# A hybrid decoder step with features on partitions in memory: input rows, gains, y and k without transpositions

## The chip, the cores and the metric

The kernel runs on one core of one Trainium2 chip. The time is the device time of one execution in microseconds. Engines are named as the profile names them: PE is TensorE's matrix multiply and PEld its weight load, DVE is VectorE, ACT is ScalarE, POOL is GpSimd, SP is SyncE, which issues most of the DMAs.

## The reference

One layer for two groups of rows that share all weights: a prompt of 256 rows and 8 samples of 4 rows, 288 rows (T) in all, each of D = 2048 features.

```
h   = RMSNorm(x, g_pre)
q, k, v, u, vg = split(h @ w_in)          # q, k rotated on the first quarter of each head of 128
A   = block-sparse attention(q, k, v)     # the samples also read 2048 cached keys and values each
B   = gelu(u) * (tril(w_spatial[g]) @ LayerNorm(gelu(vg)) + b_spatial[g])
mix = (sigmoid(h @ Wga) * (A @ w_a_out) + sigmoid(h @ Wgb) * (B @ w_b_out)) @ w_o
x   = x + RMSNorm(mix, g_post)
x   = x + RMSNorm(SwiGLU(RMSNorm(x)), g_pof)
y   = x + (p @ w_ple) * sigmoid(RMSNorm(x) @ w_ple_gate)
```

The outputs are y, the rotated k rows, the v rows and the normalised vg rows of the samples. Everything is float32.

## The kernel before

Inside the kernel every activation lies with features on partitions: a tile is 128 features by 288 rows. The inputs and outputs lie in memory by rows, so x, p, the gains, the spatial weights, y and k are turned on PE. Each transposition is one PE instruction with the identity matrix `cst`; a PSUM tile `pt` takes three (two of 128 prompt rows, one of 32 sample rows padded to 128).

**Products.** `product` (lines 237 to 260) does all the large multiplications. It takes 256 output features at a time. For each group of 4 blocks of 128 input features SP loads 512 KB of weights into one of four `wr` buffers, ACT rounds them to `wh`, DVE makes the remainder `wl`, and PE does three multiplications of 128 x 288 for each block and half: `wh` by the high part, `wh` by the low part, `wl` by the high part of the activation. There are 520 such weight groups.

**Start.** SP loads `cst` (line 134), then x in four chunks of 512 features, three tiles each (line 157); ACT loads `g_pre` in 16 rows (line 165), POOL the five other gains (line 168) after clearing the sample tiles (lines 139, 140). Ten multiplications of ones (`wake`, line 185) start PE, two PE instructions each. `h_parts` (209) turns one block into `pt`; ACT writes `hh` = g * x (215) and DVE the remainder `hl` (216) from PSUM. Two q products run along, one weight group each per chunk. `square_sums` (218) squares the untransposed rows on ACT; `r0_of` (226) makes the reciprocal root of the mean square with three diagonal matrices on PE. `rope` (300) then empties the q accumulators; it needs `r0`.

**k, v and the cache.** `k_gen` (331) turns each k tile back to rows through `to_tokens` (310: three transpositions, an ACT copy, a DVE copy) and POOL stores them (322, 323). Cached keys and values (2 MB per round of four pages) stream in on SP during some 550 us; their PE work is woven into the products by planned counts.

**Spatial weights.** `prep_gen` (458) loads them in rows of 512 bytes (462), turns eight 128 x 128 blocks on PE (469) and masks them on DVE from PSUM (470).

**Middle.** After the `w_a_out` products x is loaded again (855 to 864): four chunks `xc` with two buffers, 48 transpositions, 16 DVE copies into `x1`. The `w_o` products follow, then `p` is loaded and turned (933 to 947), which `le_products` need, then `norm_of` and `residual`.

**End.** The last products `pg` have the epilogue `pg_done` (1031). After each second group of 256 features it turns 512 features of the result with 12 transpositions (1045), copies them on ACT (1047) and stores three pieces on SP (1048).

**Order.** The framework sets the order on each engine and each DMA queue at build time, from a simulation of when operands and buffers are ready, in program order where several are. Each engine and each queue then works through its list in order: a wait holds up what stands behind it.

Of the kernel before, what the change touches and what calls it, by code (L numbers as in the profile page):

```python
# [21 lines left out]
NB = 8  # L22
# [86 lines left out]
def tile_hybrid_step(ctx: ExitStack, tc: tile.TileContext, a: dict, o: list):  # L109
    nc = tc.nc  # L110
    y_p, y_s, kp_o, vp_o, ks_o, vs_o, gv_o = o
# [20 lines left out]

    cst = perm.tile([128, 128], F32, name="cst")
# [8 lines left out]
    TP = 3 * 128  # L142

    def turn(pt, tiles, c):

        for j, t in enumerate(tiles):
            nc.tensor.transpose(pt[:, j * 128:j * 128 + 128], t[:, c], ident)

    xp = a["x_prompt"].rearrange("b s d -> (b s) d")
    xs = a["x_sample"].rearrange("b s d -> (b s) d")  # L150
    srcs = [(xp[0:128], 128), (xp[128:256], 128), (xs, TS)]
    XC = 512
    x_tok = [[p_x0.tile([128, XC], F32, name=f"x{j}_{c}") for j in range(3)] for c in range(D // XC)]

    def x_load(c):
        for (src, n), t in zip(srcs, x_tok[c]):
            nc.sync.dma_start(t[:n], src[:, c * XC:c * XC + XC])

    for tiles in x_tok:
        clear_rows(tiles[2])  # L160
    x_load(0)
    names = ["g_pre_mix", "g_post_mix", "g_pre_ffn", "g_post_ffn", "g_ple", "g_vnorm"]
    glist = [a[name].rearrange("l (k p) -> (l k) p", p=128) for name in names]
    gl0 = p_x0.tile([16, 128], F32, name="gl0")
    nc.scalar.dma_start(gl0, glist[0])
    gl = p_x0.tile([72, 128], F32, name="gl")
    for i, g in enumerate(glist[1:]):
        nc.gpsimd.dma_start(gl[16 * i:16 * i + g.shape[0]], g)
# [11 lines left out]
    def bank(shape, name, of="aux"):  # L180
        return psum[of].tile(shape, F32, name=name, tag=of)
# [27 lines left out]
    def h_parts(c):  # L209
        for i in range(XC // 128):  # L210
            k = c * (XC // 128) + i
            pt = bank([128, TP], "pt")
            turn(pt, x_tok[c], slice(i * 128, i * 128 + 128))
            pt = pt[:, :T]
            nc.scalar.activation(hh[:, k], pt, AF.Copy, scale=g_pre[:, k:k + 1])
            nc.vector.scalar_tensor_tensor(hl[:, k], pt, g_pre[:, k:k + 1], hh[:, k], op0=ALU.mult, op1=ALU.subtract)

    def square_sums(c):
        for j in range(3):
            junk = p_x0.tile([128, XC], F32, name="junk", bufs=2)  # L220
            nc.scalar.activation(junk, x_tok[c][j], AF.Square, accum_out=sums[:, j, c:c + 1])

    sums = p_x0.tile([128, 3, D // XC], F32, name="sums")
    r0 = p_h.tile([128, T], F32, name="r0")

    def r0_of():
        st = p_x0.tile([128, 3], F32, name="st")
        nc.vector.tensor_reduce(st, sums, axis=AX.X, op=ALU.add)
        r0p = bank([128, TP], "r0p")
        for j in range(3):  # L230
            dg = p_x0.tile([128, 128], F32, name="dg", bufs=3)
            nc.vector.tensor_scalar(dg, ident, st[:, j:j + 1], None, op0=ALU.mult)
            nc.tensor.matmul(r0p[:, j * 128:j * 128 + 128], ones_d, dg, start=True, stop=True)
        rstd_of(r0, r0p[:, :T], p_x0.tile([128, T], F32, name="r0t"))
# [40 lines left out]
    for c in range(D // XC):  # L275
        h_parts(c)
        for q in q2:
            next(q)
        if c + 1 < D // XC:
            x_load(c + 1)  # L280
        square_sums(c)
    r0_of()
    gains = turned_gains(gl, 72)
    g_pm, g_pf, g_pof, g_pl, g_vn = (gains[:, 16 * i:min(16 * i + 16, 72)] for i in range(5))
# [46 lines left out]
    def k_gen():  # L331
        def done(x, h):
            rope(kT[:, h:h + 2], x)
            c = p_a.tile([128, 2, GC], F32, name="k_tok", tag="a2", bufs=2)
            cs = p_a.tile([TS, GC], F32, name="ks_tok", tag="a3")
            for t in range(2):
                s = slice(t * HD, t * HD + HD)
# [93 lines left out]
    def gmlp_gen():  # L431
# [26 lines left out]
        def prep_gen():  # L458
            gm = p_g.tile([128, C_GM], F32, name="gm")
            nc.sync.dma_start(gm, a["c_gm"])  # L460
            wsp = p_g.tile([128, H, 128], F32, name="wsp", tag="vn")
# [3 lines left out]
            tri = gm[:, C_TRI:C_TRI + 128][:, None, :].to_broadcast([128, 4, 128])  # L465
            for g in range(0, H, 4):
                tp = bank([128, 4, 128], "wt")
                for t in range(4):
                    nc.tensor.transpose(tp[:, t], wsp[:, g + t], ident)
                nc.vector.tensor_tensor(wst[:, g:g + 4], tp, tri, ALU.mult)  # L470
                yield 0.5
# [382 lines left out]

    p_xt, end_xt = pool("p_xt", "left")
    for c in range(4):
        xc = [p_xt.tile([128, 512], F32, name=f"xc{j}", bufs=2) for j in range(3)]
        clear_rows(xc[2])
        for (src, n), t in zip(srcs, xc):
            nc.sync.dma_start(t[:n], src[:, c * 512:c * 512 + 512])  # L860
        for k in range(4):
            pt = bank([128, TP], "pt")
            turn(pt, xc, slice(k * 128, k * 128 + 128))
            nc.vector.tensor_copy(x1[:, 4 * c + k], pt[:, :T])
# [68 lines left out]
    pp_ = a["p_prompt"].rearrange("l b s c -> (l b s) c")  # L933
    ps_ = a["p_sample"].rearrange("l b s c -> (l b s) c")
    psrc = [(pp_[0:128], 128), (pp_[128:256], 128), (ps_, TS)]
    p_tok = [p_n.tile([128, PLE], F32, name=f"ptok{j}", tag="yt", bufs=3) for j in range(3)]
    clear_rows(p_tok[2])
    for (src, n), t in zip(psrc, p_tok):
        nc.sync.dma_start(t[:n], src)
    ph = p_n.tile([128, 2, T], F32R, name="ph")  # L940
    pl = p_n.tile([128, 2, T], F32R, name="pl")
    for k in range(2):
        pt = bank([128, TP], "pt")
        turn(pt, p_tok, slice(k * 128, k * 128 + 128))
        pt = pt[:, :T]
        nc.scalar.copy(ph[:, k], pt)
        nc.vector.tensor_tensor(pl[:, k], pt, ph[:, k], ALU.subtract)
# [15 lines left out]
    end_xt.close()  # L963
# [14 lines left out]
    for half in range(2):  # L978
# [40 lines left out]
        for g in range(8):  # L1019
# [8 lines left out]
    outs = [y_p.rearrange("b s d -> (b s) d")[0:128], y_p.rearrange("b s d -> (b s) d")[128:256],  # L1028
            y_s.rearrange("b s d -> (b s) d")]

    def pg_done(x, g):
        for t in range(2):
            m = 2 * g + t
            gt = p_f.tile([128, T], F32, name="pgt", tag="fs", bufs=4)
            nc.vector.tensor_tensor(gt, x[t], r3, ALU.mult)
            nc.scalar.activation(gt, gt, AF.Sigmoid)
            nc.vector.tensor_tensor(gt, gt, le[:, m], ALU.mult)
            nc.vector.tensor_tensor(x1[:, m], x1[:, m], gt, ALU.add)
        if g % 2 == 0:
            return  # L1040
        for j in range(3):
            n = 128 if j < 2 else TS
            pt = bank([128, 512], "yt")
            for i in range(4):
                nc.tensor.transpose(pt[:n, i * 128:i * 128 + 128], x1[:, 2 * g - 2 + i, j * 128:j * 128 + n], ident)
            yt = p_n.tile([128, 512], F32, name="yt", bufs=3)
            nc.scalar.copy(yt[:n], pt[:n])
            nc.sync.dma_start(outs[j][:, (g // 2) * 512:(g // 2) * 512 + 512], yt[:n])
# [5 lines left out]
    for end in (end_f, _x, end_z, end_n, end_banks):  # L1054
# [3 lines left out]
_INS = ["x_prompt", "x_sample", "cache_k", "cache_v", "page_table", "p_prompt", "p_sample", "g_pre_mix", "w_in",  # L1058
        "g_vnorm", "w_spatial", "b_spatial", "w_a_out", "w_b_out", "w_gate", "w_o", "g_post_mix", "g_pre_ffn",
        "w_ffn_in", "w_ffn_out", "g_post_ffn", "g_ple", "w_ple_gate", "w_ple"]  # L1060
_OUTS = [(1, SEQ, D), (NB, NS, D), (1, 1, SEQ, H, HD), (1, 1, SEQ, H, HD), (1, NB, NS, H, HD), (1, NB, NS, H, HD),
         (1, NB, NS, H * 128)]
# [25 lines left out]
```

## Time and profile before

| | us |
|---|---|
| median of 3 runs | 1848.33 (1846.85 to 1848.41) |
| the profiled execution | 1845.0 |
| its span, first to last instruction | 1843.2 |
| PE busy in the span | 1822.8 (99%) |
| DVE, ACT, POOL busy | 951.8, 775.2, 97.8 |
| granted TensorE clock, mean | 0.997 |

The span is 1.8 us shorter than the execution it belongs to. Multiplications overlap in the pipeline: one of 128 x 288 is listed with 295 ns, but the next one starts 133 ns later, so busy time is not a sum of steps, and the step from one start to the next is what an instruction costs PE. Of the runs, the profiled execution is the shortest.

### The profile page before, as it was taken

The page shows a single profiled execution, that of the slowest core. Times are in us where ns is not written, and L with a number is a line of the kernel's source. Part 1 is how long each engine was busy: PE and PEld are TensorE (multiplying, and loading weights), DVE is VectorE, ACT ScalarE, POOL GpSimd, SP SyncE. Part 2 cuts the span into 40 slices and gives each one's busy share as a digit, 9 for nine tenths or more (in the row PEclk, how much of TensorE's full clock was granted, in tenths as well). Part 3 has the DMA queues.
Part 4 walks back from the last instruction along what each step waited for, and adds up shares of the span by engine and source line. Part 5 has one row for each costly group of instructions (what it writes and reads, how often), then busy time and mean ns, then how long its engine had stood idle before and what let it go on. Part 6 is the DMA issues. An engine that isn't in the chain of part 4 may idle for free.

```text
span 1843.2 us, 38883 instructions
## 1 busy us (share of the span) xinstructions
PE 1822.8 (99%) x16004; PEld 1775.4 (96%) x16004; DVE 951.8 (52%) x1357; ACT 775.2 (42%) x1090; POOL 97.8 (5%) x195
## 2 busy tenths in 40 slices
PE   8999999999999999999999999999999999999898
PEld 8999899999999989999999999999999999999898
DVE  4754446544444347635855554433545545444764
ACT  5334455434333344445533333333333333434643
POOL 2010112000000000110000000000000000001000
PEclk9999999999999999999999999999999999999999
DMA  9589999999999985544555554445555555444452
GB/s 344 168 297 350 329 354 329 365 344 363 356 340 353 374 280 180 181 164 138 167 162 170 162 170 162 163 163 166 172 162 170 162 170 162 164 161 155 137 192 101
DMA packets 312673, 414.83 MB, mean 225 GB/s; under 512 B 13544, under 2 KB 275296, under 8 KB 312496
## 3 DMA queue, kind: packets, MB, share of 16 engines
q1 hardware_dynamic: 311120, 409.23, 64.7%
q8 instruction: 125, 2.05, 0.4%
q0 software_dynamic: 1200, 2.76, 0.4%
q10 hardware_dynamic: 176, 0.37, 0.1%
q14 instruction: 52, 0.43, 0.1%
HBM read 407.45 MB, written 4.85 MB: 224 GB/s over the span
## 4 chain that ended last, share of the span: by engine, by line
PE 97%; DVE 1%; ACT 1%; issue 0%; DMA 0%; SPq 0%; DVEq 0%
PE f L256 5%; PE f L257 5%; PE fa L257 5%; PE f L255 5%; PE fg L257 5%; PE fg L255 5%; PE fg L256 5%; PE fa L255 5%; PE fa L256 5%; PE values L732 3%; PE scores L634 3%; PE ga L255 2%; PE pg L255 2%; PE gb L255 2%; PE ga L256 2%; PE pg L257 2%
## 5 line engine op out<-in xcount | busy, mean ns | idle before, releaser
L249 DVE TENSOR_TENSOR wl<-wr,wh 128x1024 fp32r<-128x1024 f32 (+1 forms) x520 | 623.9, 1201 | 719.9 <-ACT wh L248 708.1
L248 ACT CAST wh<-wr 128x1024 fp32r<-128x1024 f32 (+1 forms) x520 | 535.8, 1031 | 896.0 <-PE f L256 165.2
L257 PE MATMUL f<-dh,wl 128*128 128x288 f32 x704 | 208.9, 297 | 0.0
L256 PE MATMUL f<-dl,wh 128*128 128x288 f32 x704 | 208.5, 296 | 0.0
L255 PE MATMUL f<-dh,wh 128*128 128x288 f32 x704 | 207.5, 295 | 0.0
L255 PE MATMUL fg<-zh,wh 128*128 128x288 f32 x704 | 207.3, 295 | 0.0
L257 PE MATMUL fg<-zh,wl 128*128 128x288 f32 x704 | 207.2, 295 | 0.0
L257 PE MATMUL fa<-zh,wl 128*128 128x288 f32 x704 | 206.7, 295 | 0.5 <-DVE wl L249 0.5
L256 PE MATMUL fa<-zl,wh 128*128 128x288 f32 x704 | 206.0, 294 | 0.9 <-DVE zl L925 0.9
L256 PE MATMUL fg<-zl,wh 128*128 128x288 f32 x704 | 206.9, 294 | 0.0
L255 PE MATMUL fa<-zh,wh 128*128 128x288 f32 x704 | 204.7, 295 | 1.0 <-ACT zh L924 1.0
L256 PEld LDWEIGHTS fa<-zl,wh 128*128 128x128 f32 x704 | 132.5, 188 | 1.2 <-DVE zl L925 1.2
L257 PEld LDWEIGHTS fa<-zh,wl 128*128 128x128 f32 x704 | 132.0, 188 | 0.7 <-DVE wl L249 0.7
L256 PEld LDWEIGHTS fg<-zl,wh 128*128 128x128 f32 x704 | 132.7, 188 | 0.1
L256 PEld LDWEIGHTS f<-dl,wh 128*128 128x128 f32 x704 | 132.6, 188 | 0.0
L255 PEld LDWEIGHTS fa<-zh,wh 128*128 128x128 f32 x704 | 131.4, 188 | 1.2 <-ACT zh L924 1.2
L255 PEld LDWEIGHTS f<-dh,wh 128*128 128x128 f32 x704 | 132.3, 188 | 0.1
L255 PEld LDWEIGHTS fg<-zh,wh 128*128 128x128 f32 x704 | 132.3, 188 | 0.0
L257 PEld LDWEIGHTS fg<-zh,wl 128*128 128x128 f32 x704 | 132.1, 188 | 0.1
L257 PEld LDWEIGHTS f<-dh,wl 128*128 128x128 f32 x704 | 132.1, 188 | 0.1
L255 PE MATMUL pg<-zh,wh 128*128 128x288 f32 x256 | 76.1, 304 | 5.4 <-ACT zh L924 5.4
L255 PE MATMUL gb<-hh,wh 128*128 128x288 f32 x256 | 76.7, 299 | 0.0
(356 smaller groups left out, 3792.2 us busy)
## 6 DMA issues: line engine op xcount, KB each, us to landing
wr<-in_w_ffn_in SPq DMA_DIRECT2D x176, 512.0 KB, 3.4
kt<-in_cache_k SPq DMA_DIRECT2D x128, 512.0 KB, 7.4
vt<-in_cache_v SPq DMA_DIRECT2D x128, 512.0 KB, 6.5
wr<-in_w_in SPq DMA_DIRECT2D x80, 512.0 KB, 6.3
wr<-in_w_ffn_out SPq DMA_DIRECT2D x80, 512.0 KB, 3.2
wr<-in_w_gate SPq DMA_DIRECT2D x64, 512.0 KB, 6.8
wr<-in_w_o SPq DMA_DIRECT2D x32, 512.0 KB, 3.2
wr<-in_w_ple_gate SPq DMA_DIRECT2D x32, 512.0 KB, 3.2
```

The source lines that it names most:

```text
L248: nc.scalar.copy(wh[:, :m], raw[:, :m])
L249: nc.vector.tensor_tensor(wl[:, :m], raw[:, :m], wh[:, :m], ALU.subtract)
L255: nc.tensor.matmul(accs[t], wh[:, i, c], xh, start=k == 0, stop=False)
L256: nc.tensor.matmul(accs[t], wh[:, i, c], xl, start=False, stop=False)
L257: late["mm"] = nc.tensor.matmul(accs[t], wl[:, i, c], xh, start=False, stop=k == n - 1)
L634: i = nc.tensor.matmul(sp[b][32 * g:32 * g + 32, 4 * n:4 * n + 4], Q[:, h2, g, dq], kt[:, :, c:c + 32], start=h2 == 1 and dq == 0, stop=h2 ...
L732: i = nc.tensor.matmul(oa[b][32 * g:32 * g + 8], w[:, n, 32 * g + 8 * part:32 * g + 8 * part + 8], v[:, :, g], start=first and part == 3, ...
```

## The change

The host passes x, p, the gains and the spatial weights with features (or the summed index) on partitions, and takes y and k in that form; it turns them itself. In the kernel all 182 transpositions of full tiles and the 2 small ones of the gains go away, with the copies that emptied them. The identity stays; v and vg are still turned.

- x: four loads of 128 x 1152 (4.6 KB per partition, 576 KB each); `hh` and `hl` read x from SBUF. `squares` works on the turned tile, 1152 elements wide, in place on ACT, and DVE adds the chunks; `r0_of` has two PE multiplications by ones.
- gains: one load of 128 x 88 (352 bytes per partition) on ACT's queue, ahead of x; `cst` moves from SP's queue to POOL's.
- k: one POOL store of 128 x 576 per group, straight from `kT`.
- spatial weights: loaded straight into `wst`, masked in place by one DVE operation of 128 x 1024.
- x again: one load of 2.36 MB into `x1` on SP; p: one load of 128 x 576, one ACT and one DVE operation.
- y: a store of 128 x 576 on SP after each group of 256 features, eight in all.

```diff
@@ start
+    xs = [p_x0.tile([128, XK, T], F32, name=f"x{c}") for c in range(KD // XK)]
+    def x_load(c):
+        nc.sync.dma_start(xs[c], a["x"][:, c * XK:c * XK + XK])
+    gains = perm.tile([128, 88], F32, name="gains")
+    nc.scalar.dma_start(gains, a["gains"])
+    x_load(0)
-    nc.sync.dma_start(cst, a["c_perm"][:, :128])
+    nc.gpsimd.dma_start(cst, a["c_perm"][:, :128])
...
-            pt = bank([128, TP], "pt")
-            turn(pt, x_tok[c], slice(i * 128, i * 128 + 128))
+            nc.scalar.activation(hh[:, k], xs[c][:, i], AF.Copy, scale=g_pre[:, k:k + 1])
...
+    def squares(c):
+        nc.scalar.activation(xs[c], xs[c], AF.Square)
+        if c:
+            nc.vector.tensor_tensor(xs[0], xs[0], xs[c], ALU.add)
...
+        nc.vector.tensor_tensor(q[:, 0:2], q[:, 0:2], q[:, 2:4], ALU.add)
+        for i in range(2):
+            nc.tensor.matmul(r0p, ones_d, q[:, i], start=i == 0, stop=i == 1)
@@ k_gen
-                to_tokens(kT[:, h + t], c[:, :, s], cs[:, s])
-            rows_out(kp_o, ks_o, h, c, cs)
+            nc.gpsimd.dma_start(k_o[:, h:h + 2], kT[:, h:h + 2])
@@ prep_gen
-            nc.sync.dma_start(wsp, a["w_spatial"].rearrange("l g t s -> t (l g) s"))
+            nc.sync.dma_start(wst, a["w_spatial"])
-                    nc.tensor.transpose(tp[:, t], wsp[:, g + t], ident)
-                nc.vector.tensor_tensor(wst[:, g:g + 4], tp, tri, ALU.mult)
+            nc.vector.tensor_tensor(wst, wst, gm[:, C_TRI:C_TRI + 128][:, None, :].to_broadcast([128, H, 128]), ALU.mult)
@@ middle
-            turn(pt, xc, slice(k * 128, k * 128 + 128))
-            nc.vector.tensor_copy(x1[:, 4 * c + k], pt[:, :T])
+    nc.sync.dma_start(x1, a["x"])
...
+    nc.sync.dma_start(p_f32, a["p"])
+    nc.scalar.copy(ph, p_f32)
+    nc.vector.tensor_tensor(pl, p_f32, ph, ALU.subtract)
@@ pg_done
-                nc.tensor.transpose(pt[:n, i * 128:i * 128 + 128], x1[:, 2 * g - 2 + i, j * 128:j * 128 + n], ident)
-            nc.scalar.copy(yt[:n], pt[:n])
-            nc.sync.dma_start(outs[j][:, (g // 2) * 512:(g // 2) * 512 + 512], yt[:n])
+        nc.sync.dma_start(y_o[:, 2 * g:2 * g + 2], x1[:, 2 * g:2 * g + 2])
```

## Rows read from the trace of the kernel before

**Rows 1.** The page: the busy line of TensorE (PE: busy us, share of the span, instructions) and the summary of the chain of work that ended last (share of the span by engine).

```profile
PE 1822.8 (99%) x16004; PEld 1775.4 (96%) x16004; DVE 951.8 (52%) x1357; ACT 775.2 (42%) x1090; POOL 97.8 (5%) x195
...
PE 97%; DVE 1%; ACT 1%; issue 0%; DMA 0%; SPq 0%; DVEq 0%
```

**Rows 2.** The busy time of each engine by stretch. Columns: the stretch and its length in us; busy us and instructions of PE, PEld (weight load), DVE, ACT and POOL; granted TensorE clock; mean busy share of the DMA engines; GB/s.

```profile
5.70:17.00 11.30, 8.79 (x60) 7.59 (x60) 6.82 (x11) 10.05 (x21) 7.06 (x16) 1.00 1.04 363
17.00:45.00 28.00, 26.91 (x201) 25.87 (x200) 13.12 (x21) 14.11 (x29) 0.00 (x0) 1.00 1.04 393
145.00:640.00 495.00, 494.88 (x5736) 461.32 (x5735) 240.42 (x423) 211.79 (x319) 40.52 (x99) 1.00 0.96 350
1716.00:1727.00 11.00, 5.64 (x38) 5.19 (x37) 8.89 (x13) 7.34 (x16) 0.00 (x0) 0.84 0.77 241
1727.00:1734.00 7.00, 7.00 (x43) 7.00 (x43) 7.00 (x14) 4.15 (x9) 0.00 (x0) 0.77 0.02 8
```

**Rows 3.** The groups of TensorE instructions by line. Columns: line, engine, operation, output and inputs, shape, count | busy us in all, mean ns of one | idle us before them and what ended it. A transposition is one MATMUL with the identity (`cst`) as an input.

```profile
L147 PE MATMUL pt<-cst,x 128*128 128x128 f32 x48 | 7.9, 286 | 2.8 <-DVE hl L216 1.5 <-DMA x<-in_x_prompt 1.2
L1045 PE MATMUL yt<-cst,x 128*128 128x128 f32 (+1 forms) x48 | 7.9, 275 | 2.0 <-DVE x L1038 1.4 <-ACT yt L1047 0.6
L147 PE MATMUL pt<-cst,xc 128*128 128x128 f32 x48 | 7.3, 272 | 0.0
...
L315 PE MATMUL tt<-cst,kT 128*128 128x128 f32 (+1 forms) x24 | 3.3, 275 | 0.0
...
L889 PE MATMUL nrm<-sq,ones_d 128*128 128x288 f32 x8 | 2.4, 405 | 0.0
```

**Rows 4.** The timeline of TensorE around the eight transpositions of the spatial weights. Columns: start us, length us, engine, line, operation, count of the merged instructions.

```profile
291.03 0.30 PE L257 MATMUL gb<-hh,wl 128*128 128x288 f32 x1
291.16 1.04 PE L469 MATMUL wt<-cst,wsp 128*128 128x128 f32 x8
...
292.17 0.30 PE L256 MATMUL gb<-hl,wh 128*128 128x288 f32 x1
292.31 0.30 PE L257 MATMUL gb<-hh,wl 128*128 128x288 f32 x1
```

**Rows 5.** The timeline of the first 13 us (SPq is the DMA-issuing SyncE). Columns as in rows 4; in brackets the idle time before and what ended it.

```profile
1.08 4.64 PE L185 MATMUL wake<-ones_d 128*128 128x128 f32 x20 [1.08 <-DVE eps L177]
1.21 0.89 SPq L157 DMA_DIRECT2D x<-in_x_prompt  x2
...
5.86 1.79 PE L147 MATMUL pt<-cst,x 128*128 128x128 f32 x9
...
6.20 0.63 ACT L221 ACTIVATE junk<-x 128x512 f32<-128x512 f32 x1 [0.88 <-DMA x<-in_x_prompt]
...
7.51 0.87 ACT L215 ACTIVATE hh<-pt,gains 128x288 fp32r<-128x288 f32 x2
...
8.28 1.04 ACT L248 CAST wh<-wr 128x1024 fp32r<-128x1024 f32 x1
...
9.37 0.40 PE L255 MATMUL q<-hh,wh 128*128 128x288 f32 x1 [0.23 <-ACT wh L248]
```

**Rows 6.** The DMA issues of the first 60 us. Columns: output and input, issuing engine, count, KB each, median us from issue to landing.

```profile
x<-in_x_prompt SPq DMA_DIRECT2D x8, 256.0 KB, 7.1
...
gl<-in_g_pre_mix ACTq DMA_DIRECT2D x1, 8.0 KB, 1.9
gl<-in_g_post_mix POOLq DMA_DIRECT2D x1, 8.0 KB, 6.1
```

**Rows 7.** Who TensorE waited for over the whole span. Columns: the waiting operation and line <- the releaser: us in all, times, longest us.

```profile
PE pg L255 <- ACT zh L924: 5.4, 1, 5.4
...
PE le L255 <- ACT ph L946: 1.4, 1, 1.4
```

**Rows 8.** Groups of VectorE instructions by line and shape, columns as in rows 3.

```profile
L922 DVE TENSOR_TENSOR x<-x,mo_f 128x576 f32<-128x576 f32 x8 | 5.9, 747 | 0.0
```

**Rows 9.** The timeline at the end of the `w_o` products. Columns as in rows 5.

```profile
857.41 0.82 PE L147 MATMUL pt<-cst,ptok 128*128 128x128 f32 x6
...
858.47 0.42 ACT L878 ACTIVATE sq<-o 128x288 f32<-128x288 f32 x1
...
859.62 1.06 PE L255 MATMUL le<-ph,wh 128*128 128x288 f32 x6 [1.40 <-ACT ph L946]
...
860.52 0.65 PE L889 MATMUL nrm<-ssq_mo,ones_d 128*128 128x288 f32 x2
```

**Rows 10.** The timeline of the end. Columns as in rows 5.

```profile
1835.23 0.60 PE L1045 MATMUL yt<-cst,x 128*128 128x128 f32 x4
...
1836.78 0.82 DVE L1038 TENSOR_TENSOR x<-x,pgt 128x288 f32<-128x288 f32 x2
...
1838.63 1.66 SPq L1048 DMA_DIRECT2D out<-yt  x3
```

**Rows 11.** The DMA issues of the last 8 us, columns as in rows 6.

```profile
out<-yt SPq DMA_DIRECT2D x2, 256.0 KB, 2.7
out<-yt SPq DMA_DIRECT2D x1, 64.0 KB, 2.2
```

**Rows 12.** The timeline of SyncE's DMA issues late in the last products. Columns as in rows 4; a merged row lasts from its first issue to its last.

```profile
1795.16 19.73 SPq L245 DMA_DIRECT2D wr<-in_w_ple_gate  x7
1816.00 24.28 SPq L1048 DMA_DIRECT2D out<-yt  x6
```

More of the change, by code (lines that the diff above doesn't have):

```diff
@@ L110, in tile_hybrid_step @@
     nc = tc.nc
-    y_p, y_s, kp_o, vp_o, ks_o, vs_o, gv_o = o
+    y_o, k_o, vp_o, vs_o, gv_o = o
     perm = ctx.enter_context(tc.tile_pool(name="perm", bufs=1, side="left"))
@@ L131, in tile_hybrid_step @@
     end_banks = banks(acc=6 - AUX, aux=AUX, long=2)
+    XK = 4
+    xs = [p_x0.tile([128, XK, T], F32, name=f"x{c}") for c in range(KD // XK)]
[3 more added lines that the diff above has]
+    nc.scalar.dma_start(gains, a["gains"])
+    g_pre, g_pm, g_pf, g_pof, g_pl, g_vn = (gains[:, 16 * i:min(16 * i + 16, 88)] for i in range(6))
+    x_load(0)
     cst = perm.tile([128, 128], F32, name="cst")
-    nc.sync.dma_start(cst, a["c_perm"][:, :128])
+    nc.gpsimd.dma_start(cst, a["c_perm"][:, :128])
     ident = cst
@@ L140, in clear_rows @@
         nc.gpsimd.memset(t[64:128], 0.0)
[L142 to L168, printed above, removed]
     pt_sb = p_kv.tile([1, NB * NPG], I32, name="pt_sb")
@@ L209, in h_parts @@
     def h_parts(c):
-        for i in range(XC // 128):
-            k = c * (XC // 128) + i
-            pt = bank([128, TP], "pt")
-            turn(pt, x_tok[c], slice(i * 128, i * 128 + 128))
[L214 to L223, printed above, removed]
+        for i in range(XK):
+            k = c * XK + i
+            nc.scalar.activation(hh[:, k], xs[c][:, i], AF.Copy, scale=g_pre[:, k:k + 1])
+            nc.vector.scalar_tensor_tensor(hl[:, k], xs[c][:, i], g_pre[:, k:k + 1], hh[:, k], op0=ALU.mult, op1=ALU.subtract)
+    def squares(c):
+        nc.scalar.activation(xs[c], xs[c], AF.Square)
+        if c:
+            nc.vector.tensor_tensor(xs[0], xs[0], xs[c], ALU.add)
     r0 = p_h.tile([128, T], F32, name="r0")
     def r0_of():
[L227 to L234, printed above, removed]
+        q = xs[0]
+        nc.vector.tensor_tensor(q[:, 0:2], q[:, 0:2], q[:, 2:4], ALU.add)
+        r0p = bank([128, T], "r0p")
+        for i in range(2):
+            nc.tensor.matmul(r0p, ones_d, q[:, i], start=i == 0, stop=i == 1)
+        rstd_of(r0, r0p, p_x0.tile([128, T], F32, name="r0t"))
     def product(w, c0, ks, part, done, name, of="acc"):
@@ L274, in tile_hybrid_step @@
     q2 = [q_gen(0), q_gen(1, "long")]
-    for c in range(D // XC):
+    for c in range(KD // XK):
         h_parts(c)
@@ L278, in tile_hybrid_step @@
             next(q)
-        if c + 1 < D // XC:
+        if c + 1 < KD // XK:
             x_load(c + 1)
-        square_sums(c)
+        squares(c)
     r0_of()
-    gains = turned_gains(gl, 72)
-    g_pm, g_pf, g_pof, g_pl, g_vn = (gains[:, 16 * i:min(16 * i + 16, 72)] for i in range(5))
     end_x0.close()
@@ L460, in prep_gen @@
             nc.sync.dma_start(gm, a["c_gm"])
-            wsp = p_g.tile([128, H, 128], F32, name="wsp", tag="vn")
-            nc.sync.dma_start(wsp, a["w_spatial"].rearrange("l g t s -> t (l g) s"))
+            nc.sync.dma_start(wst, a["w_spatial"])
             nc.sync.dma_start(brow, a["b_spatial"].rearrange("l g t -> l (g t)").to_broadcast([128, H * 128])
                               .rearrange("p (g t) -> p g t", t=128))
[L465 to L468, printed above, removed]
-                    nc.tensor.transpose(tp[:, t], wsp[:, g + t], ident)
-                nc.vector.tensor_tensor(wst[:, g:g + 4], tp, tri, ALU.mult)
-                yield 0.5
+            nc.vector.tensor_tensor(wst, wst, gm[:, C_TRI:C_TRI + 128][:, None, :].to_broadcast([128, H, 128]), ALU.mult)
+            yield 1.0
             rp = bank([128, H, NS], "rp")
@@ L930, in residual @@
         ssq[key] = [src[:, 0], src[:, 1]]
[L933 to L939, printed above, removed]
+    p_f32 = p_n.tile([128, 2, T], F32, name="p_f32")
+    nc.sync.dma_start(p_f32, a["p"])
     ph = p_n.tile([128, 2, T], F32R, name="ph")
     pl = p_n.tile([128, 2, T], F32R, name="pl")
[L942 to L947, printed above, removed]
+    nc.scalar.copy(ph, p_f32)
+    nc.vector.tensor_tensor(pl, p_f32, ph, ALU.subtract)
     w_ple = a["w_ple"].rearrange("l k c -> (l k) c")
@@ L1055, in tile_hybrid_step, with features, outputs @@
         end.close()
[L1058 to L1062, printed above, removed]
+_INS = ["cache_k", "cache_v", "page_table", "w_in", "b_spatial", "w_a_out", "w_b_out", "w_gate", "w_o", "w_ffn_in",
+        "w_ffn_out", "w_ple_gate", "w_ple"]
+_GAINS = ["g_pre_mix", "g_post_mix", "g_pre_ffn", "g_post_ffn", "g_ple", "g_vnorm"]
+_OUTS = [(128, KD, T), (128, H, T), (1, 1, SEQ, H, HD), (1, NB, NS, H, HD), (1, NB, NS, H * 128)]
+def features(prompt, sample):
+    rows = np.concatenate([prompt.reshape(SEQ, -1), sample.reshape(TS, -1)])
+    return np.ascontiguousarray(rows.reshape(T, -1, 128).transpose(2, 1, 0))
+def outputs(y, k, vp, vs, gv):
+    y = np.ascontiguousarray(np.asarray(y).transpose(2, 1, 0)).reshape(T, D)
+    k = np.ascontiguousarray(np.asarray(k).transpose(2, 1, 0))
+    return (y[:SEQ].reshape(1, SEQ, D), y[SEQ:].reshape(NB, NS, D), k[:SEQ].reshape(1, 1, SEQ, H, HD), vp,
+            k[SEQ:].reshape(1, NB, NS, H, HD), vs, gv)
 def key_blocks(c):
@@ L1086 @@
     r = _run(nc, [arrays], core_ids=[0])
-    return tuple(r.results[0][f"out_{i}"] for i in range(len(_OUTS)))
+    return outputs(*(r.results[0][f"out_{i}"] for i in range(len(_OUTS))))
```

34 lines of the change are left out of this document (5 added, 29 removed).

## The prediction

> **What bounds the kernel now.** I read the page first. PE is busy for 99% of the span and the chain of work that ended last runs through PE for 97% of it [rows 1]; the reader should see that a PE instruction taken away shortens the run unless, where it stood, something else ends last. So the second view is the busy time by stretch [rows 2]: in the cache stretch PE has no idle time but the DMA engines are 96% busy; at the start they are at 1.04 (full) and PE idles 2.5 + 1.1 us; in 1716 to 1727 PE idles 5.4 us and the clock falls. The third view gives the groups that the change removes [rows 3], the fourth what one of them costs.
>
> **One transposition.** Its listed duration, 272 to 286 ns [rows 3], overlaps with its neighbours. The product that starts at 291.03 is followed by eight transpositions at 291.16 and the second product behind them starts at 292.17; one product step is 292.31 - 292.17 = 0.14 us [rows 4]. So eight cost 292.17 - 291.16 - 0.14 = 0.87 us, 0.109 us each. The upper bound is busy time over count, 7.3 / 48 = 0.15 us [rows 3]. I take 0.109, since the rows around it show what PE really did next.
>
> **The sum**, against the profiled execution, 1845.0 us (span 1843.2).
>
> x at the start. 48 transpositions are 5.2 us. The idle time between 5.7 and 45 us is 3.6 us [rows 2]; of it 2.7 us stood before transpositions, waiting for PSUM tiles or x [rows 3], and those waits go with them. New is a wait between the last `wake` instruction (1.08 + 4.64 = 5.7) and the first product. The first chunk is the same 576 KB, now one load issued at about 0.8 instead of three from 1.21. The second of the old tiles had landed by 6.20 [rows 5], so I put the landing at 6.0. Two `hh` operations take 0.87 and a `wh` cast 1.04 us [rows 5]; the first product starts at 8.0 instead of 9.37. Of 39.3 us up to 45, PE needs 39.3 - 3.6 - 5.2 - 0.3 (a gain transposition and edges) = 30.2; after the change it needs these, 2.3 of new wait and, I assume, 1.0 of old idle: 33.5, so 5.8 us are won. `r0` costs more: four multiplications of 288 columns at 0.24 instead of six of 128 at 0.109, the 0.24 being the step of two in 0.65 us, 0.65 - 0.405 [rows 9, 3]: -0.3. DVE's three sums over 1152 elements are twice 0.75 us each [rows 8], 4.5 in all, and 0.75 for the last one of 576; DVE is busy 6.8 + 13.1 of these 39.3 us [rows 2], which covers them unless they stand just ahead of a `wl` or of `r0`: then up to 1.5. Squares on ACT are the same elements. Clearing the sample tiles leaves POOL, which nobody waited for. Together **5.5** (3 to 9). The low end is a load landing whole at 0.8 + 7.1, the median of the row tiles [rows 6], which takes 1.9 off, and 1.0 for DVE; the high end is no old idle time left and a landing 1 us earlier.
>
> Moved issues. `cst` goes to POOL's queue, where an issue took 6.1 us to land instead of 1.9 on a hardware queue [rows 6]. The first use is a DVE copy for the query spread; placed before the first `hl` it would hold DVE to 6.9, later than `hl` needs by under 1 us: 0, bound -1. Gains come in 352-byte rows on ACT's queue, landing between 1.9 and 6.1 us after issue [rows 6], so at 2.7 to 6.9; x lands at 6.0, so 0, bound -0.9. The Trainium skill, "DMA: Bandwidth & Descriptors", Specifications, wants at least 512 bytes per piece for full rate and says that shorter ones cost a read-modify-write, which speaks against this one load; by it I would take the -0.9 bound, and no row here has so short a piece to try it on.
>
> k. 24 transpositions, 2.6 us; the ACT and DVE copies had no one on PE behind them. POOL's store now waits for `rope` instead of the copies; behind it stands only the copy of `ko`, which needs the same result: 0. Spatial weights: 8, **0.9**; the DVE mask replaces two of half its width. Both lie where PE never idles: **3.5** together (0 if the DMA engines decide there, the first rival).
>
> x again. 48 transpositions without a wait [rows 3]: **5.2**. The one load of 2.36 MB takes 6.0 us at 393 GB/s [rows 2] and stands on SP's queue ahead of weight loads. Four weight buffers hold 4 x 24 x 0.133 = 12.8 us of PE work, so 0; half of them would still cover it. Its bound is the 6.0 us, if it waits at the head of the queue, for the memory of `hh` and `hl` that it takes, until the buffers are empty. DVE's copies lay beside PE.
>
> p. Six transpositions, then PE waits 1.4 us for `ph` [rows 7, 9]: 2.05 us at most. But the chain goes on through the mean square: the last square ends at 858.9, the end of products plus 1.5, while the norm's multiplication starts at 860.52, plus 3.1 [rows 9]. That can move by 1.6; I take **1.5** (0.7 to 2.1).
>
> y. 36 of the 48 lie before the last product: **3.9**. After it, the final sum ends at 1836.78 + 0.82 = 1837.6 and the span ends 5.6 us later, through transpositions, copies and three stores, the last issued about 1839.95 [rows 10]. Now one store of 288 KB follows at 1837.65, and from there a landing like that of the 256 KB stores, 2.7 [rows 11], and 1.0 of closing, which is what the old end leaves after its last landing (1839.95 + 2.2 for 64 KB). That ends at 1841.5: **1.6** (0.6 to 2.6).
>
> Sum: 5.5 + 3.5 + 5.2 + 1.5 + 3.9 + 1.6 = **21.2 us**, 1823.8 against the profiled 1845.0. That execution is 3.3 us below the median of the runs, 1848.3; from the median the same sum gives **1827 us**, which I predict. The order on every engine is planned anew, and a stretch like 1716 to 1727 can come out longer or shorter by some of its 5.4 us of idle time [rows 7]; this bound belongs to the range.
>
> **Rivals.**
>
> First, the DMA engines end last in the cache stretch and at the start: 96% and 104% busy [rows 2]. Against it: PE is never idle from 145 to 640. Then k, spatial weights and the start give nothing and 12.2 us remain: 1836.
>
> Second, the clock. `wake` steps at (4.64 - 0.43) / 19 = 0.22 us per instruction, twice 0.109, so PE starts at the lower level (1.2 of 2.4 GHz) [rows 5]. Before, transpositions follow at once at 5.86; now PE has nothing for 2.3 us. After the wait in 1716 to 1727 the granted clock was 0.84 and 0.77 over 11 and 7 us, that is some 6.7 us at half [rows 2]. The same at the start costs 3.4: 1830. For it: that one wait did it; against: it was twice as long. The Trainium skill, "TensorE: Matmul & The Clock Gate", Part 4, says that transpositions do not count as work for the clock; by it their going changes nothing there, and no row here separates the two.
>
> Third, slower. SP works in order, and a store of y waits for DVE's final sum. If the plan put each store ahead of the next group's weight loads, as the program has them, PE would stand after each group from the third to the seventh: 2.2 for the epilogue [rows 10], 0.4 for the issue, some 3 for the load and 2 for the casts, 7.6 each, 38 in all, for 1850 to 1865 with three to five stores placed so (1848.3 - 21.2 + 7.6 each); it decides from three on. Against: the last seven weight loads, those of the last two groups, are out by 1814.9, ahead of the last six stores, which start at 1816.0 [rows 12].
>
> Fourth, no change: transpositions hidden in gaps. Rows 3 show no idle time before 72 of them and PE busy throughout; little speaks for it.
>
> **How the numbers follow.** Forecast 0.72, DMA 0.16, clock 0.05, slower 0.05, no change 0.02. A difference under about 0.2%, 3.7 us, is no change. Faster is the first three, 0.93; same 0.02; slower 0.05. The forecast's own bounds (start 3 to 9, p and the end 1 either way, 5 for the new plan or for the load of x, not all at once) give 1818 to 1835; with the DMA case and its scatter the range is 1817 to 1839.
>
> **What would show it.** Right: no PE group with `cst` and `x`, `xc`, `kT`, `wsp` or `ptok`; first q product near 8 us; no wait of `le` for `ph`; the span's end some 4 us after the last sum; PE's idle time in the cache stretch still near 0. Wrong: PE waits for `kt`, `vt` or `wr` before 640 us (first rival), a granted clock under 1 between 6 and 20 us (second), PE idle near each y store (third), or new gaps at the norms.

## The result, and the profile after

The changed kernel takes 1833.87 us (median of 4 runs, 1831.92 to 1834.04), the kernel before beside it 1847.67 (1846.85 to 1848.41): ratio 0.9923 [0.9906, 0.994], 13.8 us less. A second series of the changed kernel gave 1832.97 (e13 below). The forecast was 1827.0 with 1817 to 1839: direction and range hold, the size is two thirds of the 21.2 us that were summed. The two profiled executions lie closer together, 1845.0 and 1834.04, spans 1843.2 and 1832.3, since the one of before lies below the runs beside it (over all series its runs go from 1844.28 to 1850.35); the accounts by stretch below add up to the 10.9 us between these two spans.

The page after: TensorE's busy line and the chain of work that ended last [rows 1]. There are 186 PE instructions fewer (184 transpositions and 2 for `r0`), and PE still ends the run.

```profile
PE 1805.0 (99%) x15818; PEld 1759.8 (96%) x15818; DVE 946.7 (52%) x1329; ACT 761.7 (42%) x1049; POOL 87.4 (5%) x169
...
PE 95%; DVE 1%; DMA 1%; ACT 1%; issue 0%; SPq 0%; DVEq 0%; ACTq 0%; POOLq 0%
```

Busy time by stretch after, columns as in [rows 2]; the last stretch is that of the second norm, five us earlier than before, and the one ahead of it follows the first norm.

```profile
5.70:17.00 11.30, 8.00 (x37) 7.65 (x38) 8.87 (x14) 9.73 (x15) 1.22 (x7) 0.70 1.06 380
17.00:45.00 28.00, 23.89 (x166) 22.41 (x164) 22.02 (x35) 12.42 (x17) 0.00 (x0) 0.96 1.00 362
145.00:640.00 495.00, 493.01 (x5729) 459.38 (x5728) 240.04 (x421) 212.28 (x320) 38.89 (x99) 1.00 0.98 350
861.80:868.70 6.90, 4.53 (x19) 4.53 (x20) 6.90 (x13) 4.42 (x9) 0.00 (x0) 0.51 0.38 121
1711.00:1722.00 11.00, 5.64 (x39) 5.19 (x38) 8.76 (x13) 7.33 (x15) 0.00 (x0) 0.84 0.80 250
```

Who PE waited for, whole span [rows 7]:

```profile
PE q L224 <- ACT wh L217: 5.7, 2, 3.2
PE fa L224 <- ACT zh L870: 5.4, 1, 5.4
PE pg L224 <- ACT zh L870: 5.4, 1, 5.4
...
PE values L688 <- DMA vt<-in_cache_v: 1.8, 1, 1.8
```

The reader should see three things. From 5.7 to 45 us PE is idle 3.3 + 4.1 us, against 2.5 + 1.1 before, so the start lost what its transpositions gave. In the cache stretch PE now waits once, 1.8 us for a value tile. And the first norm, where `fa` waited about 1 us before, now has the same 5.4 us wait as the second, with half the clock behind it (0.51 in 861.8 to 868.7).

**Account.** Start of the last PE instruction of a product, read from the timelines of the two kernels, and how much earlier the changed one is:

| last product of | before | after | earlier by | won or lost in between | forecast |
|---|---|---|---|---|---|
| q | 70.23 | 71.86 | -1.6 | start -1.6 | +5.5 |
| gb (cache stretch) | 497.20 | 496.19 | 1.0 | k, spatial weights +2.6 | +3.5 |
| ga | 698.79 | 697.47 | 1.3 | +0.3 | 0 |
| o | 857.27 | 851.18 | 6.1 | x again +4.8 | +5.2 |
| first fa | 868.97 | 864.17 | 4.8 | p and the norm -1.3 | +1.5 |
| f | 1713.62 | 1708.76 | 4.9 | +0.1 | 0 |
| pg | 1835.10 | 1826.36 | 8.7 | y +3.9 | +3.9 |
| end of span | 1843.2 | 1832.3 | 10.9 | end +2.2 | +1.6 |

**The start, after.** Timeline of the first 25 us (columns as in [rows 5]):

```profile
1.99 0.51 POOL L153 DMA_DIRECT2D pt_sb<-in_page_table  x1
...
5.10 1.81 ACT L186 ACTIVATE hh<-x,gains 128x288 fp32r<-128x288 f32 x4 [2.41 <-DMA gains<-in_gains]
...
7.51 1.05 ACT L217 CAST wh<-wr 128x1024 fp32r<-128x1024 f32 x1 [0.60 <-DMA wr<-in_w_in]
...
8.61 0.61 PE L224 MATMUL q<-hh,wh 128*128 128x288 f32 x1 [3.17 <-ACT wh L217]
...
8.98 0.35 SPq L552 DMA_DIRECT2D kt<-in_cache_k  x1
10.30 0.39 SPq L214 DMA_DIRECT2D wr<-in_w_in  x1
11.49 1.48 SPq L552 DMA_DIRECT2D kt<-in_cache_k  x2
...
22.32 0.39 SPq L214 DMA_DIRECT2D wr<-in_w_in  x1
```

The same rows of the kernel before:

```profile
7.96 0.50 POOL L170 DMA_DIRECT2D pt_sb<-in_page_table  x1
...
9.61 0.30 PE L256 MATMUL q<-hl,wh 128*128 128x288 f32 x1
9.75 0.30 PE L255 MATMUL q<-hh,wh 128*128 128x288 f32 x1
...
13.41 4.88 SPq L245 DMA_DIRECT2D wr<-in_w_in  x4
19.38 2.66 SPq L596 DMA_DIRECT2D kt<-in_cache_k  x3
```

x came early and the first product starts at 8.61, not 9.37. But the page table, without which SP cannot address the cached keys, is issued at 1.99 instead of 7.96: eight clearings and five gain loads no longer stand ahead of it on POOL. It takes 6.0 us to land. The first key load goes out at 8.98 instead of 19.38, and eight have gone out before the eighth weight load at 22.32, where before all four of these weight loads went first. All of it shares DMA engines that are full (1.06). The DMA issues of the first 60 us [rows 6]; the weights' median landing before was 6.5 us:

```profile
wr<-in_w_in SPq DMA_DIRECT2D x18, 512.0 KB, 8.9
kt<-in_cache_k SPq DMA_DIRECT2D x12, 512.0 KB, 10.4
...
gains<-in_gains ACTq DMA_DIRECT2D x1, 44.0 KB, 4.3
pt_sb<-in_page_table POOLq DMA_DIRECT2D x1, 0.5 KB, 6.0
```

In the chain of waits of these 60 us the longest piece is the weight load issued at 22.32:

```profile
22.32 12.32 DMA wr<-in_w_in
34.72 1.06 ACT wh L217
```

**The first norm, after** (timeline of VectorE and TensorE; [rows 9] end with the same products):

```profile
851.32 0.29 PE L224 MATMUL le<-ph,wh 128*128 128x288 f32 x1
...
857.75 0.46 DVE L175 SCALAR_TENSOR_TENSOR rt_mo<-nrm,rt_mo 128x288 f32<-128x288 f32 x1
858.25 1.23 DVE L218 TENSOR_TENSOR wl<-wr,wh 128x1024 fp32r<-128x1024 f32 x1
859.39 0.30 DVE L176 TENSOR_SCALAR rt_mo<-rt_mo 128x288 f32<-128x288 f32 x1
859.83 1.23 DVE L218 TENSOR_TENSOR wl<-wr,wh 128x1024 fp32r<-128x1024 f32 x1
860.97 0.45 DVE L177 TENSOR_TENSOR r_mo<-r_mo,rt_mo 128x288 f32<-128x288 f32 x1
...
864.17 0.61 PE L224 MATMUL fa<-zh,wh 128*128 128x288 f32 x1 [5.37 <-ACT zh L870]
```

The `le` products follow the o products at once, as hoped, and with them the next weights: VectorE then makes two remainders `wl` of the coming `fa` products between the four steps of the norm. PE gains the wait for `ph` and pays it back before `fa`.

**The end, after** ([rows 10, 11]): the final sum ends at 1828.03 + 0.82, and 288 KB land 2.2 us after issue.

```profile
1828.03 0.82 DVE L971 TENSOR_TENSOR x<-x,pgt 128x288 f32<-128x288 f32 x2
...
out<-x SPq DMA_DIRECT2D x1, 288.0 KB, 2.2
```

### The profile page after: what moved, and what is told of

Same layout as the page of the kernel before. It is cut to its first block, busy times and chain, and to the rows that moved or that the text cites. A ratio compares the mean times of both kernels' runs of the same rounds, so it can differ in the third digit from the quotient of the medians.

```text
span 1832.3 us, 38322 instructions
## 1 busy us (share of the span) xinstructions
PE 1805.0 (99%) x15818; PEld 1759.8 (96%) x15818; DVE 946.7 (52%) x1329; ACT 761.7 (42%) x1049; POOL 87.4 (5%) x169
## 4 chain that ended last, share of the span: by engine, by line
PE 95%; DVE 1%; DMA 1%; ACT 1%; issue 0%; SPq 0%; DVEq 0%; ACTq 0%; POOLq 0%
PE fa L224 5%; PE fg L224 5%; PE fa L225 5%; PE fg L225 5%; PE f L226 5%; PE f L225 5%; PE f L224 5%; PE fa L226 5%; PE fg L226 5%; PE values L688 3%; PE scores L590 3%; PE gb L224 2%; PE pg L224 2%; PE ga L224 2%; PE pg L225 2%; PE gb L226 2%
## 5 line engine op out<-in xcount | busy, mean ns | idle before, releaser
L224 PEld LDWEIGHTS fa<-zh,wh 128*128 128x128 f32 x704 | 132.7, 189 | 5.6 <-ACT zh L870 5.6
L226 PEld LDWEIGHTS fa<-zh,wl 128*128 128x128 f32 x704 | 132.7, 189 | 0.0
L225 PEld LDWEIGHTS fa<-zl,wh 128*128 128x128 f32 x704 | 132.7, 189 | 0.0
```

What stands on the lines that cost most here:

```text
L224: nc.tensor.matmul(accs[t], wh[:, i, c], xh, start=k == 0, stop=False)
L225: nc.tensor.matmul(accs[t], wh[:, i, c], xl, start=False, stop=False)
L226: late["mm"] = nc.tensor.matmul(accs[t], wl[:, i, c], xh, start=False, stop=k == n - 1)
```

## The experiments

The theory: the transpositions are worth what was forecast where PE alone decides, and the start lost its 5.5 us because cached keys went ahead of weights on SP's queue. Rivals for the start: the granted clock, and late loads whatever their order; for the norm: the plan on VectorE with or without p.

**e1: the clock at the start.** The changed kernel with `WAKE` (the multiplications of ones, 10) set to 25.

> The changed kernel with 25 instead of 10 multiplications of ones at the start, which keep PE busy until about 8.6 us. Clock theory: PE's granted clock fell to 0.50 from 8.6 to 15.3 us because PE had nothing to do between the last of these multiplications (5.5 us) and the first product (8.6 us); with PE busy there, the stretch 8.6 to 15.3 us runs at 1.00 and half of 6.7 us, 3.3 us, comes back: about 1830.5 us against 1833.9. Rival, late loads: the products wait for x and the weights whatever the clock is, the 3.3 us turn into waits for loads: 1833 to 1834.

1832.54 us (1832.18 to 1833.79), ratio to before 0.9921 [0.9908, 0.9935]. Busy time by stretch of the changed kernel:

```profile
8.60:15.30 6.70, 6.30 (x25) 5.95 (x26) 5.67 (x9) 5.77 (x8) 0.00 (x0) 0.50 1.07 383
15.30:35.00 19.70, 19.68 (x145) 19.24 (x145) 14.58 (x21) 10.49 (x17) 0.00 (x0) 1.00 1.04 390
```

and of e1:

```profile
8.60:15.30 6.70, 6.29 (x49) 6.06 (x49) 5.67 (x9) 6.35 (x9) 0.00 (x0) 1.00 1.06 381
15.30:35.00 19.70, 18.45 (x132) 17.54 (x132) 14.64 (x21) 10.85 (x17) 0.00 (x0) 1.00 1.05 390
```

The clock did fall, to 1.2 GHz, and the longer start of PE keeps it at 2.4: 49 instructions instead of 25. Of the 24 won at once 13 are lost again in the next stretch, to waits for weights, and the last q product is only 0.8 us earlier (71.09). The loads set the pace, the clock cost little here.

**e2: keys behind the weights.** The loads of the first four pages of keys are issued after the eighth weight load; each later page follows the fourth one before it, as it did.

```diff
+            else:
+                st.enter_context(tc.issue_after(late["wr"][7].ins))
             r = nc.sync.value_load(pt_sb[...])
```

> The changed kernel with the first loads of cached keys put behind the eighth weight load on SP's queue, as they stood in the kernel before; nothing else. Queue theory: weight loads that stand behind cached keys landed 12.3 us after issue, PE waited 2.5 + 1.1 us for them near 42 us, and the clock fell to 0.51 from 42.5 to 49.5 us; without it some 3 us of waits and 3.3 us of half clock come back: about 1828 us against 1833.9. Rival, bandwidth: the DMA engines are full until 43 us in either order, so the keys come later and the waits move: 1833 to 1834.5.

1823.52 us (1823.22 to 1824.23), ratio 0.987 [0.9855, 0.9885]. SyncE's issues and PE's stretch in e2:

```profile
10.43 7.83 SPq L214 DMA_DIRECT2D wr<-in_w_in  x4
19.34 3.78 SPq L555 DMA_DIRECT2D kt<-in_cache_k  x4
```

```profile
15.30:35.00 19.70, 19.70 (x151) 19.70 (x150) 14.99 (x18) 11.55 (x17) 0.00 (x0) 1.00 1.06 381
35.00:50.00 15.00, 15.00 (x112) 14.79 (x111) 12.39 (x21) 5.60 (x6) 0.00 (x0) 1.00 1.03 359
```

No idle time from 15.3 to 50, and the last q product at 64.61: 7.25 us earlier than in the changed kernel, 5.6 earlier than before, where the forecast had said 5.5. In the changed kernel PE was idle for 4.1 us between 30 and 45 us, behind late weights, and ran at a granted clock of 0.51 from 42.5 to 49.5; both are gone, and the 7.25 us hold them together. The DMA engines are no less busy than in the changed kernel (1.06 against 1.04 from 15.3 to 35): the order of the loads did it. The other part of the 10.4 us by medians is not the start's (e13, e14).

**e3: the start alone on the kernel before** (x, gains, squares, `cst` and the queues as changed, the rest as before).

> The kernel before with the part of the change at the start alone (x and gains with features on partitions, cst on POOL's queue); k, spatial weights, x again, p and y as before. By the prediction's sum this part wins 5.5 us: 1842 against 1847.7. By the comparison of the two traces, where the last q product ended 1.6 us later than before, it loses: 1848 to 1850. Rival, the loss belongs to the new plan of the whole kernel and not to this part: 1842 to 1845.

1844.32 us (1843.63 to 1846.32, 11 runs), ratio 0.9983 [0.9974, 0.9992]. Its trace has the changed kernel's start: first key load at 8.90, last q product at 71.28. So the loss belongs to this part and not to the others; but the expected slowdown is not there, and the time lies in the range that the rival named. By runs the part is worth 3.2 us (1.5 to 4.8 by the interval), by the traces up to the last q product it costs 1.05. I had taken the loss from one trace of before, which lies below most of its runs. The two measures differ by 4 us: e3 has the faster step described with e13, worth up to 2, and e7 below shows how 1.8 can hang on which execution of before was traced. How the untraced runs of before started is not on record.

**e9: k and the spatial weights alone**, on the kernel before.

> The kernel before with k stored and the spatial weights loaded with features on partitions, nothing else changed. Theory: 24 + 8 transpositions at 0.109 us where TensorE has no idle time, 3.5 us: 1844.0. Rival (the DMA engines end last in the cache stretch): within 0.5 us of before, 1847 to 1848, with new waits for keys or values. In between, 1845 to 1846, a new wait of about 2 us for a value tile, as in the changed kernel.

1842.94 us (1841.41 to 1845.21, 10 runs), ratio 0.9976 [0.9966, 0.9985], 4.4 us by the ratio; in the trace the last gb product starts at 493.58, 3.6 earlier than before: the 3.5 of the sum. PE waits for no value tile here; the DMA engines do not decide.

**e7: x again and y alone**, on the kernel before.

> The kernel before with two parts of the change alone: the second load of x in one piece without transpositions, and y stored with features on partitions. Theory (terms add): the terms that the trace of the changed kernel bears out, 4.8 to 5.2 for x, 3.9 for y before the last product and 1.6 to 2.2 after it, together 10.3 to 11.3; from 1847.5 that is 1836 to 1837. Rival (the plan gives part of it back at the norms, as in the changed kernel): 1838 to 1841.

1837.63 us (1836.53 to 1837.64), ratio 0.9941 [0.9924, 0.9957]: 10.9 us by the ratio, as summed. Its trace bears out the terms one by one against that of before: x again 4.7, y 3.9, the end 2.4. Behind the first norm it loses 1.8, as the rival had it, and the time stands between the two expected ranges.

It shows one thing more. The start of e7 is that of before, instruction for instruction, and yet its first products follow each other by 0.24 us (9.99 to 10.23), where before has 0.14 (9.61 to 9.75). The same 6 us of before and of e7:

```profile
9.50:15.50 6.00, 4.76 (x34) 4.36 (x35) 4.08 (x6) 5.25 (x12) 3.30 (x9) 1.00 1.07 383
```

```profile
9.50:15.50 6.00, 5.69 (x22) 4.98 (x22) 3.38 (x5) 4.31 (x12) 3.36 (x9) 0.50 1.06 381
```

The last q product of e7 starts at 71.98, not at 70.23; e9, the third trace of this start, has the full clock and 70.2. So executions of one and the same start differ by 1.8 us, and the -1.6 in the account is against the better kind. Against e7 the changed start (71.86) is level.

**e4: the remainders at the norm held back.** The `wl` of the first products behind each norm are put after the first sum `x + mo_f`.

```diff
+                if hold is not None:
+                    st.enter_context(tc.issue_after(hold.ins))
                 nc.vector.tensor_tensor(wl[:, :m], raw[:, :m], wh[:, :m], ALU.subtract)
```

> The changed kernel with DVE's remainders of the first weights behind each residual (fa, fg, pg) put behind the first residual sum; nothing else. Order theory: at both residuals DVE did two to three such remainders of 1.23 us in the middle of the five steps of the reciprocal root, so that PE waited 5.4 us twice and the clock fell to half for 6.8 us after each; with the chain unbroken each wait is 2.5 us or more shorter and the falls may go: 1834 - 5 to 8, so 1826 to 1829. Rival: the chain through ACT and PE (squares, norm, le copies) ends as late anyway: 1833 to 1834; or the remainders are then late themselves and PE waits for wl instead: 1834 to 1836.

1832.38 us (1831.12 to 1833.39), ratio 0.9919 [0.9906, 0.9933]. Who PE waited for in e4:

```profile
PE fa L228 <- DVE zl L876: 2.8, 1, 2.8
PE fa L227 <- ACT zh L875: 2.6, 1, 2.6
```

One wait of 5.4 us became two, 2.6 and 2.8, and at the second norm 2.5 and 2.9: the three remainders now stand ahead of the second sum. The rival, that the work is late wherever it stands, fits.

**e6: p turned on PE as before**, in the changed kernel.

> The changed kernel with p loaded in rows and turned on TensorE as before. Theory (p): the six transpositions and the wait of `le` for `ph` kept the `le` products inside the wait for the norm, and without them the wait of the first `fa` for `zh` (5.4 us) and the fall of the clock behind it came up; with p turned again the stretch from the last o product to the first fa is 11.7 us as before instead of 13.0, the wait of fa for zh is about 1 us, and the kernel takes some 1.3 us or more less than the changed one, 1830 to 1832.5. Rival (plan): the order of VectorE at the norm comes from the plan whatever p does; then the remainders still stand between the steps of the norm and the run is 0.5 to 2 us longer than the changed one, 1834.5 to 1836.

1832.47 us (1831.85 to 1833.6), ratio 0.9917 [0.99, 0.9933]. VectorE and the first `fa` of e6:

```profile
854.36 0.46 DVE L174 TENSOR_TENSOR rt_mo<-r_mo 128x288 f32<-128x288 f32 x1 [2.36 <-ACT r_mo L173]
...
855.70 0.46 DVE L177 TENSOR_TENSOR r_mo<-r_mo,rt_mo 128x288 f32<-128x288 f32 x1
...
860.55 0.80 PE L224 MATMUL fa<-zh,wh 128*128 128x288 f32 x4 [0.95 <-ACT zh L870]
```

The four steps of the norm stand together again, within 1.8 us instead of 4.2, the wait for `zh` is 0.95 instead of 5.37, and the last o product (848.86) to the first `fa` takes 11.69 us, as before (11.70), against 12.99 in the changed kernel. With its six transpositions, its copies and its wait for `ph` the old p was 1.3 us cheaper here. The runs lie 0.5 to 1.4 us below the two series of the changed kernel, too little to tell by themselves; the trace decides.

**e8, e11, e12: can more be had on top of e2?** e8 is e2 with `WAKE` 25, e11 is e2 with p turned, e12 is e2 with the remainders held until the second `zl`.

> The changed kernel with both edits to the start: the first load of cached keys is issued after the eighth weight load, and 25 multiplications of ones instead of 10. Theory (clock hidden by late loads): with the weights in time the fall of the clock from 8.6 to 15.3 us is no longer covered, so the longer start of TensorE is now worth its 3.3 us and the kernel takes some 1820.3. Rival: the first two products wait for x and weights in any case, and the run is within 1 us of the one with the held load alone, 1822.5 to 1824.

1824.3 us (1823.53 to 1826.8), ratio 0.9869 [0.9852, 0.9885]: nothing. The last q product of e8 starts at 66.89, later than e2's; PE waits 3.0 us for remainders instead.

> The changed kernel with the held first load of cached keys and p turned on TensorE as before. Theory (p's early products set the remainders between the norm's steps): beside the run with the held load alone (1823.5) the stretch from the last o product to the first fa falls from 13.0 to 11.7 us, its clock no longer falls, and the run takes 1.3 to 3 us less, 1820.5 to 1822.2. Rival (p's effect was scatter of the plan): 13.0 us stay and the six transpositions cost 0.7 more, 1824.

1824.65 us (1824.13 to 1825.49), ratio 0.9878 [0.9862, 0.9895].

> The changed kernel with the held first load of cached keys, and VectorE's remainders of the first products behind each norm held until the first two remainders of the activation (`zl`) are out, not only behind the first sum. Theory: the earlier hold failed because three remainders (3.49 us) stood ahead of the second sum; with zl in front of them the first fa starts at o end + 10.4 and its second step about 1.3 us later instead of 4, and each of the two norms ends 1.5 to 2.5 us sooner: 1818.5 to 1820.5. Rival: TensorE then waits for the held remainder wl instead of zl, and the run is within 1 us of the one with the held load alone, 1822.5 to 1824.5.

1823.76 us (1823.22 to 1825.69), ratio 0.9873 [0.9857, 0.989]. In the traces both theories hold: from the last o product to the first `fa` 11.68 us in e11 and 10.26 in e12, against 12.99 in e2. In the time neither is there. At the first `fa` e11 is 0.9 and e12 1.2 us ahead of e2; at the last f product they are 2.2 and 2.1 behind. Two of these 3.2 us stand in the next pair.

**e13, e14: the changed kernel and e2 a second time.**

> The changed kernel itself a second time, for one number: how many TensorE instructions start in 1160 to 1540 us, a stretch without a wait or a fall of the clock. Its first profile has 2862 there (380 / 2862 = 132.8 ns a step), like before; the runs with the held load of cached keys or the held remainders have 2870 (132.4 ns), worth 2.0 us over the 690 us of the fa, fg and f products. Theory (the step belongs to an execution, not to a kernel): a second profile can show 2870, and then a time some 2 us below the other. Rival (it belongs to the kernel's order): 2862 again and 1831.9 to 1834.

> The changed kernel with the held first load of cached keys a second time, beside the changed kernel on the same chip. If the step belongs to an execution, 2862 or 2870 instructions in 1160 to 1540 us, and the difference to the changed kernel lies between the 7.3 us that the trace shows at the last q product and 10.4; if it belongs to the kernel's order, 2870 again and 1823.2 to 1824.2.

1832.97 us (1832.39 to 1833.85), ratio 0.9918 [0.9904, 0.9932], and 1823.91 (1823.66 to 1825.32), ratio 0.9872 [0.9857, 0.9887]. PE instructions in 1160 to 1540 us, then granted clock, DMA share and GB/s; one row each of the changed kernel, e2 and e12:

```profile
1160.00:1540.00 380.00, 380.00 (x2864) 1.00 0.53 166
```

```profile
1160.00:1540.00 380.00, 380.00 (x2872) 1.00 0.53 167
```

```profile
1160.00:1540.00 380.00, 380.00 (x2865) 1.00 0.53 167
```

The repeats have 2864 and 2872 again. (The view counts two more than the expectation does, those that overlap its ends.) As far as two repeats can show, the step belongs to the kernel as built, not to the execution: 132.7 ns in the changed kernel and e12, 132.3 in e2, with no wait and the full clock in either. Over the 690 us of fa, fg and f products that is 2.0 us. e2 beat the changed kernel by 9.1 us in this pair: 7.4 at the last q product (64.47 against 71.88) and about 2 by the step. e11 and e12 lack those 2 us, so their gain at the norm does not show beside e2; e4 has them (2873), so its 1.5 us need nothing from the norm.

## Why the prediction was right and where its size was wrong

**Right, by its own steps.** The price of one transposition, 0.109 us, held wherever PE had no other limit: k and spatial weights 3.6 against 3.5 (e9), x again 4.8 against 5.2, y 3.9 against 3.9, the end 2.2 against 1.6 (within 0.6 to 2.6). e7 shows the last three by themselves, 10.9 us by runs and 4.7, 3.9 and 2.4 in its trace. The forecast's own figures for the end, 1837.65 + 2.7 + 1.0, make 1841.35 and not 1841.5, so the term should have been 1.85, nearer to the 2.2. The first rival, DMA engines ending last, got one wait of 1.8 us for a value tile in the cache stretch, and e9 has none; k and the spatial weights gave 2.6 of their 3.5 in the changed kernel. Its other half, a start that gives nothing, is what came, but e2 wins the start back with the DMA engines as busy: the order decided. The third, y stores ahead of weights, did not come: PE waits for no weights among the `pg` products.

**The mis-sized step: the start, forecast +5.5 (3 to 9), in the trace -1.6.** That is 7.1 of the 10.3 us by which the two profiled spans fall short of the sum. Against e7's execution of the old start it is +0.1, and the 3.2 us of e3 by runs leave some 1.2 if 2.0 are its faster step: the measures go from -1.6 to +1.2, so the start gave about nothing and its sign is not settled. The forecast looked at PE's own waits and took the queues as they were: "Clearing the sample tiles leaves POOL, which nobody waited for." On POOL behind the clearings stood the page table, and SP's key loads need it. The step of the argument that fails is that work taken from an engine nobody waits for changes nothing: it let other transfers start 10 us earlier, into DMA engines that [rows 2] showed full. e2 shows it: with the keys behind the weights the start gives 5.6 (7.4 against e7). That the early page table is what moved the keys is read from the rows (8.0 landing, 8.98 first key load, in the changed kernel; nearly the same in e3) and was not tried by delaying the table alone.

**The second rival's condition came true, its price did not.** The clock was at half for 6.7 us of the first products, as that rival said; it named 3.4 us, but e1 won 0.8 in the trace and e8 nothing, since PE then waited for weights or remainders. All nine traces of the changed start with ten multiplications of ones begin their products with steps of 0.24 us; e1 and e8, with 25 of them, have the full clock there.

Whether the transpositions had kept the clock up before stays open. The Trainium skill, "TensorE: Matmul & The Clock Gate", Part 4, says that transpositions do not count as work for the clock. In the trace of before, the transpositions that follow `wake` start 0.21 us apart up to 6.55 and 0.11 us apart from 7.05 on, and the products behind them run at the full clock, as in e9. In e7 the same transpositions start 0.11 us apart up to 7.59, but 0.18 and 0.21 apart from 8.81 on, and the products run at half. Two traces against one: with transpositions the first products met either level, and no run changes them alone.

**The wrong sign: p, forecast +1.5 (0.7 to 2.1), measured -1.3.** The wait for `ph` went, as written. Late next were VectorE's remainders: `le` no longer waits, so its weight buffers come free sooner and the remainders of `fa` are ready in the middle of the norm. e6 and e11 show that p's part alone does this; the steps in between are read from the rows. The text's bound of 5 us for a changed stretch at a norm had room for it; the term's own range did not.

The gains' load of 352-byte rows landed 4.3 us after issue, between the 1.9 and 6.1 of the bounds; `hh` waited 2.4 us for it, but the first cast of weights waited for its load until 7.51 all the same, so the late gains cost PE nothing. The Trainium skill, "DMA: Bandwidth & Descriptors", Specifications, asks for at least 512 bytes per piece for full rate; no run here has this load in longer pieces.

Against the median of the runs the same account looks milder: 13.8 won of 21.2. The profiled execution of before is 2.7 us below its median, and taking a sum made in one execution from the median of others adds that difference without a term for it; e7 shows that the start alone can make 1.8 us of it. By runs the parts tried alone give 3.2 + 4.4 + 10.9 = 18.5 us; less e3's faster step (2.0) and p (1.3) that is 15.2, against 14.2 and 15.2 by the ratios of the two series of the changed kernel; each part has an interval of 1.7 to 3 us either way.

That 1833.87 lies within the range is in part luck: the range was wide for other causes, the DMA case at 1836 and a new plan. The forecast had listed what would show it wrong, and three of these signs came: a wait for `vt` before 640 us, the clock under 1 between 6 and 20 us, and a new gap at a norm.

## What to carry to other kernels

Work taken off an idle engine's queue moves everything behind it forward; follow it to the transfers that it releases, and ask what they will crowd out. When inputs arrive sooner, fix the order of the loads by hand: one line that kept the cached keys behind the eighth weight load was worth more than half of the whole change. Before a difference of 2 us in one stretch is put down to a change, look at a second execution of the unchanged stretch. Where a chain of small steps on VectorE decides, a wait ahead of it on another engine may be what keeps other work out of it.

## What was not expected of the hardware

- One and the same start met the full clock at its first products in two executions (before, e9) and half of it in a third (e7: 0.50 in 9.5 to 15.5 us, 22 instructions instead of 34).
- The step of the same 128 x 288 product in an unbroken stretch at full clock is 132.7 ns in some builds and 132.3 in others, the same in each repeat (2864 and 2872 instructions in 380 us): about 2 us of 690, as much as several edits here. What sets it is open.
- The granted clock that a row lists for the first microseconds can be too high: in 9.20 to 13.26 us of e2 it is 1.00, while 16 instructions take 4.06 us, 0.25 each, and 16 more take 2.04 us behind them. There the step tells the level, not the clock column.

```profile
9.20:13.26 4.06, 4.06 (x16) 1.00 1.07 367
13.26:15.30 2.04, 2.04 (x16) 1.00 1.03 406
```
